# Hybrid decoder block: LRU, q, k and gate projections first, as 2x2 block products with seven multiplications

## The chip, the cores and the metric

The kernel runs on one core of a Trainium2 chip. The metric is the device time of one execution in microseconds (us); before the change it is 2504.58 us, the median of three runs. The engines are named as in the profile: PE (TensorE matmul), PEld (its weight load), DVE (VectorE), ACT (ScalarE), POOL (GpSimd) and SP (SyncE, whose queue starts nearly all DMAs here).

## The reference, cut to what matters

```python
D_MODEL = 1024; SEQ = 2048; N_HEADS = 8; HEAD_DIM = 64; V_DIM = 128
SPLIT_SIZES = (D_RNN, D_RNN, D_QK, D_QK, D_ATTN, D_ATTN, 2 * D_MODEL)   # 8192 columns
u = rmsnorm(h, pre_g[l])
z = jnp.einsum('bsd,df->bsf', u, w_in[l])
xr, zr, q, k, v, za, gm = jnp.split(z, split_points, axis=-1)
xc = causal_depthwise_conv(xr, conv_w[l], conv_b[l])
y_r = rg_lru(xc, ...) * jax.nn.silu(zr)            # recurrence over the 2048 positions
o = diff_attention(qh, kh, vh, lam)                # per head: softmax(q0 k0) - lam * softmax(q1 k1), causal, times v
o = rmsnorm(o, subln_g[l]) * (1.0 - lam_init)
y_a = o.reshape(B, S, D_ATTN) * jax.nn.silu(za)
g_r, g_a = jnp.split(jax.nn.sigmoid(gm), 2, axis=-1)
m = (g_r * jnp.einsum('bse,ed->bsd', y_r, w_br_rnn[l])
     + g_a * jnp.einsum('bse,ed->bsd', y_a, w_br_attn[l]))
h = h + rmsnorm(jnp.einsum('bsd,de->bse', m, w_out[l]), post_g[l])
```

## The kernel before, in words

Every product with weights is made in fp16 with two halves: a float32 value is scaled by a power of two and split into a high part and the rest, and high x high, high x rest and rest x high are summed in PSUM. So a projection of 128 output channels over 512 positions is 8 blocks of the inner dimension x 3 = 24 matmuls of 128x512 (`mm3`, L187 to L194). The normalised input lies in SBUF, transposed and split, as `uT` [128, 2, 8, 2048]; its 16 tiles of 128 positions are turned by two DMA transposes each (`x_fin`, L276), all issued from SP's queue.

The program has three stages.

1. The LRU stage. For 8 blocks of 128 channels `xr_half` and `zr_half` project half a row (1024 positions) of x_r and z_r, and convolution, gates (float32r matmuls L351 to L353), scan and gating run on DVE, ACT and POOL. The first three blocks are made in pieces of 128 positions (L302 to L304), so that the PE can start on each tile of the input as it comes.
2. The attention stage. An attention unit is one head and 128 queries (t = 0 to 15; unit t has t + 1 key blocks). `a_scores` makes the scores of the two softmaxes (ci = 0, 1) in pieces of up to 1024 keys (L814), and DVE copies each piece out of PSUM with its maximum (L826, with the mask L830). `a_exp` takes bias `nb` (L845) and the exponentials on ACT (L851). `a_comb` of the unit before joins the two softmaxes on DVE (L874), makes the high part on ACT (L876) and the rest on POOL (L877), and two DMA transposes per piece give `pt` (L880). `a_pv` multiplies `pt` with v two units later (L897, `LAG`), and after four units `a_norm` normalises. Between these parts the loop puts projection groups out of the list `fills`: k and q of 512 positions (`g_k`, `g_q`: 24 matmuls, a split on ACT and DVE (L667, L668), then DMAs that move the parts into `K` and `Q`), v and z_a of 256 positions (`g_va`: 48 matmuls of 128x256, L711) and the merge gates (`g_gm`: 24 matmuls and a tanh, stored to DRAM `gm_d`). A running count `acc` says how many groups are due in a unit, and `need` what a unit can't do without. Eight of the gate groups are kept for the end (`GM_T`).
3. The last stage, for two halves of the positions: the branch projections with the merge (`branch`, L1094) and the output projection with norm and residual (`final`, L1125).

Tile pools set which tile may be written when; a scheduler orders each engine's instructions when the program is built, so the order on an engine is not that of the source text. It is fixed at build time, and every engine runs its list in order.

Of the kernel before, what the change touches and what calls it, by code (L numbers as in the profile page):

```python
# [23 lines left out]
NH = 8  # L24
# [7 lines left out]
PD = 5     # x tiles loaded ahead  # L32
# [3 lines left out]
SEG_A = 2  # where a head's gate projections stand between its chunks  # L36
SEG_B = 5
# [11 lines left out]
def kernel(  # L49
# [35 lines left out]
    gm_d = drp.tile([2 * KD, 128, S], F32, name="gm_d")  # L85

# [3 lines left out]
    w16_p = ctx.enter_context(tc.tile_pool(name="w16", bufs=1))  # L90
# [3 lines left out]
    with ExitStack():  # L94
# [38 lines left out]
        def w16_at(i):  # L133
            """one of the four places for a block of weights"""
            return lambda w: w16_p.tile([128, 2, KD, 128], F16, tag=f"w{i % 4}", name="w16")

        def wkey_col(key):
            nm, h = key
            return {"k": C_K, "q": C_Q, "v": C_V, "za": C_ZA, "gm": C_GM}[nm] + h * 128
# [20 lines left out]
        def w_scale(w, ps, fac, keep=None):  # L160
            """power of two that brings the block's norm close to 2^13 (a rough sum is enough for it)"""
# [6 lines left out]
            if keep is None:  # L168
                w.cz = wn_p.tile([128, 1], F32, tag=f"w_cz_{w.tag}", name="w_cz",
                                 bufs={"wg": 4, "agm": 3}.get(w.tag, 2))  # L170
                nc.vector.scalar_tensor_tensor(out=w.cz, in0=w.iv, scalar=fac, in1=cu, op0=ALU.mult, op1=ALU.mult)

        def w_fin(w, ps, fac, dst, keep=None):
            if w.sg is None:
                w_scale(w, ps, fac, keep)
            w.t = dst(w)
            nc.scalar.activation(w.t[:, 0], w.st, AF.Identity, scale=w.sg)  # L177
            nc.vector.scalar_tensor_tensor(out=w.t[:, 1], in0=w.st, scalar=w.sg, in1=w.t[:, 0],  # L178
                                           op0=ALU.mult, op1=ALU.subtract)
            w.st = None  # L180

# [1 line left out]
        utx = ExitStack()  # L183
        utp = utx.enter_context(tc.tile_pool(name="utp", bufs=1))
        uT = utp.tile([128, 2, KD, S], F16, name="uT")

        def mm3(ps, w, c0, n):  # L187
            """ps[f128, n] += w^T u over all of d, s in [c0, c0 + n)"""
            i = 0
            for k in range(KD):  # L190
                for a, b in ((0, 0), (0, 1), (1, 0)):
                    nc.tensor.matmul(ps, w.t[:, a, k, :], uT[:, b, k, c0:c0 + n],  # L192
                                     start=(i == 0), stop=(i == 3 * KD - 1))
                    i += 1  # L194

        # ================= RG-LRU branch =================
        with ExitStack() as lx:
            le = lx.enter_context(tc.tile_pool(name="le", bufs=2))
            lp = lx.enter_context(tc.tile_pool(name="lp", bufs=2))
            ly = lx.enter_context(tc.tile_pool(name="ly", bufs=2))  # L200
            lc = lx.enter_context(tc.tile_pool(name="lc", bufs=1))
            tny[0] = lx.enter_context(tc.tile_pool(name="tnl", bufs=5))
            lps = lx.enter_context(tc.tile_pool(name="lps", bufs=3, space=PSUM))
            lpt = lx.enter_context(tc.tile_pool(name="lpt", bufs=2, space=PSUM))
# [7 lines left out]
            def load_g():  # L212
                gr = le.tile([KD, 128], F32, tag="rows", bufs=1, name="gr")
                nc.scalar.dma_start(out=gr, in_=pre_g[0].rearrange("(k p) -> k p", p=128))
                gb = lp.tile([128, D], F32, tag="a", name="gb")
                nc.sync.dma_start(out=gb, in_=pre_g[0:1, :].to_broadcast([128, D]))
                return gb, gr

            def prep_g(gr):
                """power of two that keeps the scaled, normalised input in fp16's range"""  # L220
                ss, tot = tl(1, "g_ss"), tl(1, "w_tot")
                jk = le.tile([KD, 128], F32, tag="idt", bufs=1, name="jg")
                nc.scalar.activation(jk, gr, AF.Square, accum_out=ss[0:KD])
                ps = lpt.tile([128, 1], F32, tag="tot", name="tot")
                nc.tensor.matmul(ps[:, 0:1], ones[0:KD, :], ss[0:KD], start=True, stop=True)
                nc.vector.tensor_scalar(out=tot, in0=ps[:, 0:1], scalar1=1e-30, scalar2=None, op0=ALU.max)
                pow2_bits(gi, tot, 10)
                pow2_inv(cu, gi)

            xts = {}  # L230
# [3 lines left out]
            def load_x(i):  # L234
                if i >= S // 128:
                    return
# [972 lines left out]
```

## Time and profile before

| | |
|---|---|
| time, three runs | 2504.58 us median (2501.92 to 2505.71) |
| profiled execution | span 2506.1 us from its first to its last instruction; no other time is recorded for it |
| PE busy | 2353.1 us (94% of the span) |
| DVE busy | 1548.4 us (62%) |
| ACT busy | 1224.6 us (49%) |
| POOL busy | 679.7 us (27%) |
| first matmul of a projection | 17.95 us |
| first attention score | 488.4 us |
| last product with v starts | 1956.9 us |
| first matmul of the branch projections | 1996.1 us |

A group of instructions in the profile reads: line, engine, operation, tile written <- tiles read, shape, count | busy time in us, mean ns of one | idle time of the engine just before them and what ended it. The mean of a matmul is its length from start to end, and matmuls overlap, so what one costs is the busy time over the count. A row of windows gives for a stretch of time the busy time of each engine with its number of instructions, the clock granted to TensorE (1.00 is full), the share of the DMA engines and GB/s.

### The profile page before, as it was taken

Reading aid. Unit: us, or ns where it says so; the run is one execution under the profiler, and the core shown is the slowest. Engines: PE = TensorE matmul, PEld = TensorE weight load, DVE = VectorE, ACT = ScalarE, POOL = GpSimd, SP = SyncE. Lnnn points to the kernel's source line nnn. Section 1 sums busy time; section 2 is a strip of 40 time slices with the busy share of each in tenths; the row PEclk is TensorE's granted clock in tenths of the full one; section 3 lists DMA queues with packets and bytes.
Section 4 is the critical chain, followed back from the end, with each engine's and each line's share of the span. In section 5 each row is a group of like instructions: output and inputs, shape, how many; then the busy total and the mean of one; then the engine's idle time right before and its main releaser. Section 6 shows DMA issues by size and latency. Waiting matters only on the chain. (4 is left out here: it accounts for less than half of the span.)

```text
span 2506.1 us, 41430 instructions
## 1 busy us (share of the span) xinstructions
PE 2353.1 (94%) x15240; PEld 1355.3 (54%) x15240; DVE 1548.4 (62%) x4316; ACT 1224.6 (49%) x2156; POOL 679.7 (27%) x415
## 2 busy tenths in 40 slices
PE   6789999999998999998998999999999899999998
PEld 5344444465665665665665655655655444444443
DVE  8877667668658566667567478468467244633323
ACT  5555545456547546556456457356456244312211
POOL 3443334212222212222222222223123133322211
PEclk9899999999999999999999999999999999999999
DMA  9511111235444534635535445445445854743202
GB/s 244 104 43 48 46 42 34 76 81 119 108 96 111 113 84 108 127 82 113 115 84 114 103 96 118 95 90 124 95 90 115 251 177 135 239 148 118 84 17 101
DMA packets 541323, 268.73 MB, mean 107 GB/s; under 512 B 370504, under 2 KB 518016, under 8 KB 541120
## 3 DMA queue, kind: packets, MB, share of 16 engines
q1 hardware_dynamic: 538144, 256.74, 42.6%
q0 software_dynamic: 2816, 9.08, 1.2%
q8 instruction: 119, 1.95, 0.3%
q14 instruction: 84, 0.69, 0.1%
q10 hardware_dynamic: 160, 0.27, 0.0%
HBM read 110.79 MB, written 41.94 MB: 61 GB/s over the span
## 5 line engine op out<-in xcount | busy, mean ns | idle before, releaser
L192 PEld LDWEIGHTS <-w 128*128 128x128 f16 x5040 | 475.9, 100 | 576.5 <-issue 89.2
L192 PE MATMUL mm<-uT,w 128*128 128x512 f16 x3072 | 705.1, 383 | 12.9 <-ACT gm L728 8.9
L877 POOL TENSOR_TENSOR e<-e,e 128x1024 f16<-128x1024 f32 (+2 forms) x192 | 317.0, 1666 | 970.6 <-ACT e L876 487.0
L851 ACT ACTIVATE e<-e,nb,sc_h 128x1024 f32<-128x1024 f32 (+7 forms) x384 | 376.1, 980 | 160.8 <-DVE nb L845 125.6
L826 DVE TENSOR_SCALAR_CACHE_REDUCE e<-sc 128x1024 f32<-128x1024 f32 (+7 forms) x352 | 305.2, 880 | 134.9 <-PE sc L814 122.3
L192 PE MATMUL ps<-uT,w 128*128 128x512 f16 (+1 forms) x1968 | 354.4, 345 | 26.1 <-ACT xr L318 17.7
L711 PE MATMUL mm<-wva,uT 128*128 128x256 f16 x3072 | 352.7, 275 | 3.3 <-DVE st L668 2.6
L1094 PE MATMUL psb<-yt,w 128*128 128x512 f16 x1536 | 332.9, 379 | 2.0 <-ACT w L177 1.5
L711 PEld LDWEIGHTS <-uT 128*128 128x128 f16 x3072 | 301.5, 99 | 48.8 <-issue 2.9
L814 PE MATMUL sc<-K,Q 128*128 128x512 f16 (+3 forms) x1280 | 287.2, 351 | 19.9 <-DVE e L826 13.8
L897 PE MATMUL o<-V,pt 128*128 128x128 f16 x3264 | 224.5, 222 | 38.4 <-DMA pt<-e 38.1
L1094 PEld LDWEIGHTS <-w 128*128 128x128 f16 x1536 | 149.1, 98 | 184.9 <-issue 3.9
L897 PEld LDWEIGHTS <-pt 128*128 128x128 f16 x3264 | 200.0, 99 | 72.8 <-DMA pt<-e 46.5
L876 ACT ACTIVATE e<-e 128x1024 f16<-128x1024 f32 (+2 forms) x192 | 150.1, 802 | 143.1 <-DVE e L874 118.5
L814 PEld LDWEIGHTS <-Q 128*128 128x128 f16 x1280 | 119.6, 99 | 133.2 <-issue 20.2
L874 DVE SCALAR_TENSOR_TENSOR e<-e,rs,e 128x1024 f32<-128x1024 f32 (+2 forms) x192 | 190.0, 1017 | 2.2
L1125 PE MATMUL psf<-wo,m 128*128 128x512 f16 x720 | 155.7, 379 | 0.0
L156 ACT ACTIVATE jk<-wst 128x1024 bf16<-128x1024 f32 x80 | 84.2, 1052 | 138.7 <-DMA wst<-in_w_in_dram 102.6
L1125 PEld LDWEIGHTS <-m 128*128 128x128 f16 x768 | 75.1, 98 | 90.6
L1098 DVE SCALAR_TENSOR_TENSOR t<-gt,psb 128x512 f32<-128x512 f32 x64 | 43.8, 686 | 120.2 <-PE psb L1094 100.1
L1148 ACT ACTIVATE jk<-psf 128x1024 bf16<-128x1024 f32 x15 | 15.4, 1024 | 134.0 <-PE psf L1125 69.4
L717 DVE SCALAR_TENSOR_TENSOR V<-mm,V 128x256 f16<-128x256 f32 x64 | 26.9, 421 | 85.7 <-ACT V L716 85.6
(247 smaller groups left out, 2417.3 us busy)
## 6 DMA issues: line engine op xcount, KB each, us to landing
wst<-in_w_in_dram SPq DMA_DIRECT2D x64, 512.0 KB, 4.5
xt<-in_x_dram SPq DMA_DIRECT2D x32, 512.0 KB, 4.5
gm_d<-gm SPq DMA_DIRECT2D x64, 256.0 KB, 2.7
gt<-gm_d SPq DMA_DIRECT2D x32, 512.0 KB, 3.8
K<-st SPq DMA_DIRECT2D x128, 64.0 KB, 2.0
Q<-st SPq DMA_DIRECT2D x64, 128.0 KB, 2.4
Q<-st SPq DMA_DIRECT2D x128, 64.0 KB, 2.1
ya_d<-yT SPq DMA_DIRECT2D x64, 128.0 KB, 2.0
```

Of the source, the lines that this page charges most:

```text
L156: nc.scalar.activation(jk, w.st, AF.Square, accum_out=ss)
L192: nc.tensor.matmul(ps, w.t[:, a, k, :], uT[:, b, k, c0:c0 + n], start=(i == 0), stop=(i == 3 * KD - 1))
L711: nc.tensor.matmul(ps[:, j, :], uT[:, a, k, s0:s0 + 128], wt[:, b, k].rearrange("p t f -> p (t f)"), start=(i == 0), stop=(i == 3 * KD - 1))
L814: nc.tensor.matmul(ps[:, x * 128:x * 128 + m], Qt[h, t // 4][:, v, ci, q0:q0 + 128], K[:, ci, 0:m], start=(v == 0), stop=(v == 1))
L826: nc.vector.tensor_scalar(out=ev[:, 0:m], in0=ps[:, 0:m], scalar1=1.0, scalar2=None, op0=ALU.mult, op1=ALU.max, accum_out=u.mx[:, ci, col: ...
L851: nc.scalar.activation(ev[:, 0:nb * 128], ev[:, 0:nb * 128], AF.Exp, bias=nb_[:, ci:ci + 1], scale=sc_h[h], accum_out=u.sm[:, pi, ci:ci + 1])
L874: nc.vector.scalar_tensor_tensor(out=e0[:, 0:m], in0=e1v[:, 0:m], scalar=rs, in1=e0[:, 0:m], op0=ALU.mult, op1=ALU.add)
L876: nc.scalar.activation(e1[:, 0, 0:m], e0[:, 0:m], AF.Copy)
L877: nc.gpsimd.tensor_tensor(out=e1[:, 1, 0:m], in0=e0[:, 0:m], in1=e1[:, 0, 0:m], op=ALU.subtract)
L897: nc.tensor.matmul(o, pt[:, a, kb % 8, :], V[:, kb % 4, b, :], start=(kb == 0 and i == 0), stop=(kb == n - 1 and i == 2))
L1094: nc.tensor.matmul(ps, w.t[:, p, k, :], y_t[b][:, q, k, sl], start=(i == 0), stop=(i == 3 * KD - 1))
L1125: nc.tensor.matmul(pn[n], m16[:, a, j, ms], wo[:, b, j, ns], start=(j == 0 and a == 0 and b == 0), stop=(j == KD - 1 and a == 1))
```

## The change

The projections of x_r, z_r, q, k and of all merge gates are made ahead of the attention, and v and z_a alone are left to the attention stage as groups between the units.

Two blocks of 128 output channels, two halves of the inner dimension (512 each) and two runs of 512 positions form a 2x2 block product. It is made with seven block products in place of eight, on sums and differences: of the weights (A11, A12, A22, S1 to S4) and of the input (B11, B21, B22 and T1 to T4). One block product is 4 x 3 = 12 matmuls of 128x512 (`prod`), so one group has 84. There are 24 pairs of channel blocks (8 for the LRU, 8 for k and q, 8 for the gates) and two halves of the positions (p = 0, 1), 48 groups. In a group, PSUM tile Y takes four products one upon the other and ACT copies it out three times on the way (`ev`); Z takes two, X one, and DVE adds the copies to X and Z (`add_to`).

The input is kept as `uK[p]` (B11, B21, B22) and `uM[p]` (T1 to T4) for each half. For two tiles of positions that belong together (`u_pair`), four split tiles are made and turned by eight DMA transposes, two of them half as wide as the others; the block B12, which only v and z_a need, goes to DRAM (`b12_d`) and is turned and read back (`ub12`) when the first stage is over. k and q are stored to DRAM (`kq_d`), and the heads load `K` and `Q` from there (`load_kq`), four units ahead. The high parts of k, q and v are scaled by 2^-12 (`SH`), not 2^-14. The weights lie in tiles of half a block (`wq`, ten buffers), also in the last stage.

```diff
-GM_T = 8
 LAG = 2
-ACC0 = 8.0
+ACC0 = 4.0
...
+        uK = [utp.tile([128, 2, 12, CH], F16, name=f"uK{p}") for p in range(2)]
...
+            uM = [um.tile([128, 2, 16, CH], F16, name=f"uM{p}") for p in range(2)]
...
+            def u_pair(p, i):
...
+                ua = u_split(a, nc.gpsimd)
+                for l in range(2):
+                    nc.sync.dma_start_transpose(out=uK[p][:, l, 0:8, sl], in_=ua[:, l])
+                ub = u_split(b, nc.vector)
+                for l in range(2):
+                    nc.sync.dma_start_transpose(out=uK[p][:, l, 8:12, sl], in_=ub[:, l, CH:D])
+                    nc.sync.dma_start(out=b12_d[l, p * CH + i * 128:p * CH + (i + 1) * 128, :], in_=ub[:, l, 0:CH])
...
+                ua = u_split(a, nc.vector)
+                for l in range(2):
+                    nc.sync.dma_start_transpose(out=uM[p][:, l, 0:8, sl], in_=ua[:, l])
+                ub = u_split(b, nc.gpsimd)
+                for l in range(2):
+                    nc.sync.dma_start_transpose(out=uM[p][:, l, 8:16, sl], in_=ub[:, l])
...
+            pairs = [pair_of("G", 0), pair_of("K", 0), pair_of("L", 0)]
+            for i in range(1, KD):
+                pairs += [pair_of("L", 1)] if i == 1 else []
+                pairs += [pair_of("G", i), pair_of("K", i)]
+                if i + 1 < KD:
+                    pairs += [pair_of("L", i + 1)]
...
+            def prod(ps, r, p, a, b, start, stop):
+                t, k0 = ublk(p, b)
+                q = r.q[a]
+                i = 0
+                for k in range(4):
+                    for x_, y_ in ((0, 0), (0, 1), (1, 0)):
+                        nc.tensor.matmul(ps, q[:, x_, k, :], t[:, y_, k0 + k, :], start=start and i == 0,
+                                         stop=stop and i == 11, skip_group_check=True)
+                        i += 1
...
+            def g_P1(g):
+                g.Y = pY.tile([128, CH], F32, tag="Y", name="psY")
+                prod(g.Y, g.r, g.p, "A11", "B11", True, True)
+                g.y1 = ev(g.Y)
+            def g_P56(g):
+                g.Z = pZ.tile([128, CH], F32, tag="Z", name="psZ")
+                prod(g.Z, g.r, g.p, "S1", "T1", True, True)
+                prod(g.Y, g.r, g.p, "S2", "T2", False, True)
+                g.u2 = ev(g.Y)
+            def g_P27(g):
+                X = pX.tile([128, CH], F32, tag="X", name="psX")
+                prod(X, g.r, g.p, "A12", "B21", True, True)
+                add_to(g, 0, X, g.y1)
+                prod(g.Y, g.r, g.p, "S3", "T3", False, True)
+                u3 = ev(g.Y)
+                add_to(g, 3, g.Z, u3)
+            def g_P43(g):
+                prod(g.Y, g.r, g.p, "A22", "T4", False, True)
+                c_use(g, 2, g.Y)
+                prod(g.Z, g.r, g.p, "S4", "B22", False, True)
+                add_to(g, 1, g.Z, g.u2)
...
-            def g_k(h, c):
-            def g_q(h, c):
-            def g_gm(f, c):
+            def load_kq(h, c):
+                s0 = c * CH
+                t = kp.tile([128, 2, CH], F16, tag="K", name="K")
+                for l in range(2):
+                    nc.sync.dma_start(out=t[64 * l:64 * l + 64], in_=kq_d[0, h, l, :, s0:s0 + CH].rearrange(
+                        "(i p) s -> p i s", i=2))
...
             def chunk_groups(h, c):
-                return [("k", h, c), ("q", h, c), ("va", h, c, 0), ("va", h, c, 1)]
+                return [("va", h, c, 0), ("va", h, c, 1)]
...
+            fills = W_(0) + chunk_groups(0, 0) + chunk_groups(0, 1)
             for h in range(NH):
+                fills += chunk_groups(h, 2) + chunk_groups(h, 3) + W_(h + 1)
                 if h + 1 < NH:
+                    fills += chunk_groups(h + 1, 0) + chunk_groups(h + 1, 1)
...
-            per = (len(fills) - ntail - 8) / float(NH)
+            per = (len(fills) - 4) / float(NH)
+            load_kq(0, 0)
             fill_to(need[0, 0])
             for i, u in enumerate(units):
                 fill_to(need[u.h, u.t // 4])
+                if u.t % 4 == 0 and i + 4 < len(units):
+                    load_kq(units[i + 4].h, units[i + 4].t // 4)
```

Two places of the build order show how the change moves instructions. The first is SP's queue while the input is made ready. `uT`, `uK0`, `uM0` are written by DMA transposes out of split tiles `u16`, `xt` are tiles of the input, `b12_d` is the block in DRAM. Before:

```order
L240 DMA xt_215<-in_x_dram 128x1024
L276 DMA_TRANSPOSE uT_82<-u16_212 128x8x128
L276 DMA_TRANSPOSE uT_82<-u16_260 128x8x128
L276 DMA_TRANSPOSE uT_82<-u16_268 128x8x128
L240 DMA xt_263<-in_x_dram 128x1024
```

and with the change, for one pair of tiles:

```order
L235 DMA xt_359<-in_x_dram 128x1024
L235 DMA xt_361<-in_x_dram 128x1024
L262 DMA_TRANSPOSE uK0_84<-u16_404 128x8x128
L265 DMA_TRANSPOSE uK0_84<-u16_409 128x4x128
L262 DMA_TRANSPOSE uK0_84<-u16_404 128x8x128
L266 DMA b12_d_61<-u16_409 128x512
L265 DMA_TRANSPOSE uK0_84<-u16_409 128x4x128
L266 DMA b12_d_61<-u16_409 128x512
L277 DMA_TRANSPOSE uM0_91<-u16_425 128x8x128
L262 DMA_TRANSPOSE uK1_85<-u16_549 128x8x128
L274 DMA_TRANSPOSE uM0_91<-u16_420 128x8x128 x2
L277 DMA_TRANSPOSE uM0_91<-u16_425 128x8x128
```

Where two transposes stood for a tile, eight stand for a pair of tiles, and two stores beside them.

The second place is the PE's list in a late unit of a head (t = 14). `sc` are scores, `mm` are projections (L192 before), `o` is the product with v. Before, with weight loads left out:

```order
L814 MATMUL sc_10513<-K_9718,Q_9824 128x384
...
L192 MATMUL mm_10619<-uT_82,w16_10030 128x512
...
L897 MATMUL o_10563<-V_8417,pt_10348 128x128
...
L192 MATMUL mm_10619<-uT_82,w16_10030 128x512
...
L814 MATMUL sc_10539<-K_8147,Q_9824 128x512
...
L814 MATMUL sc_10546<-K_9718,Q_9824 128x384
```

and with the change, from the second softmax of t = 13 to that of t = 14:

```order
L862 MATMUL sc_20762<-K_18823,Q_20160 128x512
...
L945 MATMUL o_20401<-V_20042,pt_20667 128x128
...
L862 MATMUL sc_20769<-K_20157,Q_20160 128x256
...
L862 MATMUL sc_20861<-K_18823,Q_20160 128x512
...
L862 MATMUL sc_20868<-K_20157,Q_20160 128x384
...
L945 MATMUL o_20918<-V_19216,pt_20753 128x128
...
L862 MATMUL sc_20894<-K_18823,Q_20160 128x512
```

The 20 projection matmuls between the scores of the first and of the second softmax are gone, and no group of v and z_a stands in the units t = 11 to 14 of this head: its eight groups stand in t = 2 to 10.

More of the change, by code (lines that the diff above doesn't have):

```diff
@@ L210 @@
             gi = cst.tile([128, 1], F32, name="gi")
[L212 to L228, printed above, removed]
@@ L243 @@
[L243 to L254 removed]
+            gr = evp.tile([KD, 128], F32, tag="Y", name="gr")
+            nc.scalar.dma_start(out=gr, in_=pre_g[0].rearrange("(k p) -> k p", p=128))
@@ L280 @@
-            order = [(C_XR if i % 2 == 0 else C_ZR) + (i // 2) * 128 for i in range(2 * KD)]
-            ahead = [("k", 0), ("q", 0), ("v", 0), ("za", 0)]
-            order += [wkey_col(k) for k in ahead]
-            ws = {}
-            def wld(i):
-                ws[i] = w_load(win, order[i], tag="wg" if i < 2 * KD else "a" + ahead[i - 2 * KD][0])
-            def wstat(i):
-                w_stat(ws[i])
-            def wfin(i):
-                w_fin(ws[i], lpt.tile([128, 1], F32, tag="tot", name="tot"), 0.5 if i % 2 and i < 2 * KD else 1.0,
-                      w16_at(i))
@@ L311 @@
[L311 to L325 removed]
+                a, b = xts.pop(n), xts.pop(n + 1)
@@ new lines, in g_P43, with after, tick @@
+            def g_P43(g):
[3 more added lines that the diff above has]
+                add_to(g, 1, g.Z, g.u2)
+            later = []
+            clock = [0]
+            def after(n, f):
+                later.append((clock[0] + n, f))
+            def tick():
+                clock[0] += 1
+                for e in [e for e in later if e[0] <= clock[0]]:
+                    later.remove(e)
+                    e[1]()
@@ L454 @@
-            x_stat(6, 2)
-            x_fin(6, 2, gb)
-            wld(3)
-            x_stat(8, 2)
-            x_fin(8, 2, gb)
-            wstat(3)
-            wfin(3)
-            prm_ps = lpt.tile([128, 65], F32, tag="tot", name="prm_ps")
+            gb = lp.tile([128, D], F32, tag="y", name="gb")
+            nc.sync.dma_start(out=gb, in_=pre_g[0:1, :].to_broadcast([128, D]))
+            for n in range(2, 4):
+                load_x(n)
+            p_load(pairs[0])
+            load_x(4)
@@ new lines @@
+            g_ss, g_tot = tl(1, "g_ss"), tl(1, "w_tot")
+            g_jk = evp.tile([KD, 128], F32, tag="Y", name="g_jk")
+            nc.scalar.activation(g_jk, gr, AF.Square, accum_out=g_ss[0:KD])
+            g_ps = gps(1)
+            nc.tensor.matmul(g_ps, ones[0:KD, :], g_ss[0:KD], start=True, stop=True)
+            nc.vector.tensor_scalar(out=g_tot, in0=g_ps, scalar1=1e-30, scalar2=None, op0=ALU.max)
+            pow2_bits(gi, g_tot, 8)
+            pow2_inv(cu, gi)
+            u_pair(0, 0)
@@ new lines, with u_blk @@
+            while later:
+                tick()
+        ubp = utx.enter_context(tc.tile_pool(name="ubp", bufs=1))
+        ub12 = [ubp.tile([128, 2, 4, CH], F16, name=f"ub12{p}") for p in range(2)]
+        for p in range(2):
+            for l in range(2):
+                for i in range(4):
+                    nc.sync.dma_start_transpose(out=ub12[p][:, l, :, i * 128:(i + 1) * 128],
+                                                in_=b12_d[l, p * CH + i * 128:p * CH + (i + 1) * 128, :])
+        def u_blk(l, k, s0):
+            p, c, o = s0 // HALF, (s0 // CH) % 2, s0 % CH
+            if c == 0:
+                return uK[p][:, l, k, o:o + 128]
+            return uK[p][:, l, 4 + k, o:o + 128] if k >= 4 else ub12[p][:, l, k, o:o + 128]
@@ L594 @@
             ps_m = ax.enter_context(tc.tile_pool(name="ps_m", bufs=2, space=PSUM))
-            wl = {k: ws[2 * KD + i] for i, k in enumerate(ahead)}
+            wl = {}
             wva_t = {}
```

671 lines of the change are left out of this document (324 added, 347 removed).

## The prediction

> **What bounds the kernel now.** I read the page, then windows by stage, then groups and waits inside the attention, then the timeline at the joints.
>
> ```profile
> span 2506.1 us, 41430 instructions
> PE 2353.1 (94%) x15240; PEld 1355.3 (54%) x15240; DVE 1548.4 (62%) x4316; ACT 1224.6 (49%) x2156; POOL 679.7 (27%) x415
> 0.00:120.00 120.00, 76.78 (x726) 56.75 (x727) 100.14 (x253) 61.95 (x86) 42.94 (x38) 0.90 0.82 180
> 120.00:488.00 368.00, 347.49 (x1556) 168.30 (x1554) 264.19 (x307) 197.69 (x186) 137.09 (x72) 0.97 0.13 41
> 488.00:1975.00 1487.00, 1415.31 (x10577) 897.91 (x10578) 974.61 (x3230) 834.30 (x1700) 364.43 (x228) 0.98 0.49 107
> 1975.00:2506.00 531.00, 513.56 (x2384) 232.32 (x2382) 209.48 (x528) 130.63 (x185) 135.26 (x77) 0.99 0.43 138
> ```
>
> The windows are start, the rest of the LRU stage, attention, last stage; the columns PE, PEld, DVE, ACT, POOL, clock, DMA share, GB/s. The PE is 94% to 97% busy in every stage but the start. In the attention DVE works 975 of 1487 us, and that is hidden because the PE has projections to do meanwhile:
>
> ```profile
> L192 PE MATMUL mm<-uT,w 128*128 128x512 f16 x3072 | 705.1, 383 | 12.9 <-ACT gm L728 8.9
> L192 PE MATMUL ps<-uT,w 128*128 128x512 f16 (+1 forms) x1968 | 354.4, 345 | 26.1 <-ACT xr L318 17.7
> L711 PE MATMUL mm<-wva,uT 128*128 128x256 f16 x3072 | 352.7, 275 | 3.3 <-DVE st L668 2.6
> L1094 PE MATMUL psb<-yt,w 128*128 128x512 f16 x1536 | 332.9, 379 | 2.0 <-ACT w L177 1.5
> L814 PE MATMUL sc<-K,Q 128*128 128x512 f16 (+3 forms) x1280 | 287.2, 351 | 19.9 <-DVE e L826 13.8
> L897 PE MATMUL o<-V,pt 128*128 128x128 f16 x3264 | 224.5, 222 | 38.4 <-DMA pt<-e 38.1
> DVE e L826 <- PE sc L814: 122.3, 79, 4.8
> DVE s L862 <- ACT e L851: 83.0, 39, 5.1
> ```
>
> The 3072 matmuls `mm` (k, q, gates), 705 us, lie between the attention's own work. The last two rows (who waited for whom in the attention: total, times, longest) say that DVE waits for scores and exponentials and the PE hardly for DVE.
>
> **The change part by part.**
>
> *Fewer products.* 4608 matmuls of 512 columns (3072, and 1536 for x_r and z_r) become 48 x 84 = 4032. The 576 saved cost between 0.217 us (L1094: 332.9 / 1536) and 0.2365 us (LRU stage: 368 / 1556, all waits in it): 125 to 136 us off the PE. That is the whole gain; what follows is what stands against it.
>
> *The first stage.* It has 4032 + 192 gate matmuls. I take 0.2365 us each, since the LRU work that set that rate runs here too: 999 us; at 0.217 it would be 917. Not all can run from the start: the order has group 1 (p = 0), 12 matmuls of the next pair, and then products on `uK1`, `uM1`, which exist when the last of 16 input tiles is turned. Before, the PE started on the first tile:
>
> ```profile
> 17.95 0.26 PE L192 MATMUL ps<-uT,w 128*128 128x128 f16 x1 [2.90 <-DMA uT<-u]
> 13.40 1.35 SPq L276 DMA_TRANSPOSE uT<-u  x1
> 71.88 25.88 SPq L276 DMA_TRANSPOSE uT<-u  x10
> uT<-u SPq DMA_TRANSPOSE x32, 4.9
> ```
>
> 32 transposes took SP from 13.4 to 97.8 us, 2.64 us each with the input loads between them, and the last landed 4.9 us later. With the change there are 48 whole and 16 half ones, 56 wholes: 13.4 + 56 x 2.64 + 4.9 = 166 us. If SP's 1.35 us for one is the price, 64 of them end at 105 us: the lower bound. I take 166: the ten of the second row stand with almost nothing between them and still took 2.6 us.
>
> The Trainium skill, DMA: Bandwidth & Descriptors, section Latency and other measured facts, gives 261 GB/s for a DMA transpose; by that one of these (256 KB) would take an estimated 1.0 us, 56 of them 56 us, and the stage and the sum would be 92 us shorter. The rows above stand against it.
>
> Until 166 us the PE can do some 120 matmuls (28 us). The stage then ends at 166 + 999 - 28 = 1137 us; 1137 against 488 before. The conversions (`ev`, `add_to`) go beside the PE: one group has six of them at about 0.7 us in 19.9 us. What is late if that cover is gone is a rival below.
>
> *The joint.* The 16 half transposes of B12 wait for the end of the stage, and the loads of K and Q stand behind them on SP; weights of v and z_a have to be split. At 1.35 us the 16 take 22 us, and two groups of v on the first chunk (2 x 48 x 0.115 = 11 us) go meanwhile. No row shows it; ends 0 and 30 us, I take 12.
>
> *The attention.* Taken out: 1536 matmuls of k and q, most of the gates' 1536, and on DVE
>
> ```profile
> L668 DVE SCALAR_TENSOR_TENSOR st<-mm,st 128x512 f16<-128x512 f32 x61 | 41.7, 685 | 54.5 <-ACT st L667 54.5
> L178 DVE SCALAR_TENSOR_TENSOR w<-wst,w_sg_agm,w 128x1024 f16<-128x1024 f32 x16 | 23.8, 1487 | 0.8 <-ACT w L177 0.7
> L178 DVE SCALAR_TENSOR_TENSOR w<-wst,w_sg_ak,w 128x1024 f16<-128x1024 f32 x7 | 9.5, 1355 | 0.2 <-ACT w L177 0.2
> L178 DVE SCALAR_TENSOR_TENSOR w<-wst,w_sg_aq,w 128x1024 f16<-128x1024 f32 x7 | 8.9, 1278 | 0.1
> L164 DVE TENSOR_SCALAR w_tot<-tot 128x1 f32<-128x1 f32 x44 | 6.7, 153 | 3.0 <-PE tot L162 3.0
> ```
>
> that is 42 + 24 + 18 us, and some 30 us of small steps (30 blocks x 7 x 0.15). DVE keeps 975 - 114 = 861 us. The PE keeps 353 + 287 + 225 = 864 us. And one unit waits for the one before: bias, exponentials, join, maxima of the second softmax, next bias. Where little is projected, the spacing of the biases shows that loop:
>
> ```profile
> 1397.41 0.28 DVE L845 TENSOR_SCALAR nb<-mx,nsc_h,lsp 128x2 f32<-128x2 f32 x1
> 1400.86 0.29 DVE L845 TENSOR_SCALAR nb<-rm,nsc_h,lsp 128x2 f32<-128x2 f32 x1
> 1548.31 0.28 DVE L845 TENSOR_SCALAR nb<-rm,nsc_h,lsp 128x2 f32<-128x2 f32 x1
> 1558.68 0.29 DVE L845 TENSOR_SCALAR nb<-rm,nsc_h,lsp 128x2 f32<-128x2 f32 x1
> 1530.00:1560.00 30.00, 25.45 (x186) 14.64 (x185) 25.66 (x81) 20.12 (x38) 8.45 (x5) 0.94 0.60 122
> ```
>
> 3.45 us from t = 0 to 1, 10.4 us from t = 14 to 15; the mean, 6.9 us, over 128 units is 886 us. So the stage has three floors of nearly one height, 861, 864 and 886 us, and no spare work to lay over the gaps of each: in t = 11 to 14 no v or z_a is left, and the PE has there some 0.44 us per key block (287 + 225 us over 8 x 136), 5 to 7 us a unit, against 9 to 10.4 us of the loop. The window above, t = 13 to 15 of one head, is the stretch of before nearest to this: DVE was busy 25.66 of 30 us, 86%. I take that share for the stage: 861 / 0.86 = 1001 us, against 1487 before. Ends: 886 (the loop alone) and 1148 (DVE busy 75%).
>
> *The last stage.* Before, eight gate groups filled the time in which the last unit is normalised, stored and read back:
>
> ```profile
> 1954.38 2.74 PE L897 MATMUL o<-V,pt 128*128 128x128 f16 x46
> 1962.82 2.50 SPq L929 DMA_TRANSPOSE yT<-y  x2
> 1970.42 5.45 SPq L1025 DMA_DIRECT2D yt<-yr_d  x4
> 1996.08 12.00 PE L1094 MATMUL psb<-yt,w 128*128 128x512 f16 x54 [1.50 <-ACT w L177]
> yt<-yr_d SPq DMA_DIRECT2D x8, 1024.0 KB, 10.1
> ```
>
> That cover is gone. From the end of the last product (1957.1) to the issue of `yt` are 13.3 us and 10.1 more to its landing: 23 us of idle PE. From 1996.1 the stage runs 510 us as before. 533 us; ends 520 and 545.
>
> *Sum:* 1137 + 12 + 1001 + 533 = 2683 us of span. The span of the profiled execution, 2506.1 us, is 1.5 us over the median of the three runs (2504.58), so the time is about 2682 us, 177 us slower.
>
> **The rivals.**
>
> *The PE stays the bound (faster).* The first stage at 0.217 us: 166 + 917 - 26 = 1057; the attention at the loop's floor, 886; a joint hidden; 525 for the rest: 2468 us. For it speaks that the PE was never short of work before; against it that DVE reached 86% in a stretch where the PE still had projections. It decides where first score and attention together take less than 1967 us (2500 - 533). Chance 0.07.
>
> *Both stages better than I take, yet slower.* Ramp at 130 us and attention at 920 us (DVE 94%): 2566 us. Chance 0.17. With it the gain just fails to pay for ramp and idle gaps.
>
> *DVE holds up the first stage.* In the LRU stage DVE worked 264 of 368 us, for about 13 of 16 half rows some 20 us each; a group with 84 matmuls has 19.9 us of PE. In the 16 LRU groups DVE also has `add_to` (3 x 0.7) and weights to split, and the PE waits for X and Z behind convolution and scan. 5 us in each of 16 groups: 80 us, 2762 us. Against it: the 32 other groups leave DVE two thirds idle, and work is put off over later groups. Chance 0.13.
>
> *The clock falls.* With gaps on the PE the granted clock drops:
>
> ```profile
> 71.00:98.00 27.00, 18.30 (x72) 0.00 (x0) 0.82 0.67 127
> ```
>
> 0.82 while the PE waited for transposes. If it fell to 0.82 in t = 0 to 10, where the PE has about 61 us a head (29 us of its own, 32 us of v and z_a), that would be 13 us a head, 104 us: 2786 us. Against it: 0.94 in the window of t = 13 to 15. Chance 0.06.
> By the Trainium skill, TensorE: Matmul & The Clock Gate, section What's actually happening, the array runs at half clock after an idle window of about 3.4 us and at full clock after as long a busy one; the gaps of 4 us per late unit are at that limit, which is why this rival has a chance.
>
> **How the numbers follow.** The forecast of 2682 us has 0.57. Its own range is 2600 to 2770 (ramp -60, attention -80 to +70, the rest 20). To hold eight in ten I reach down to 2550, past the better case (2566), and up to 2830, past both slower rivals; out are the faster rival and the tail in which both slower ones meet (2866). 0.2% is about what a measurement of this kernel can tell from no change. Faster 0.07, same 0.02 (a point between the faster rival and the better case), slower 0.91.
>
> **What would show it.** In the profile of the changed kernel: about 4032 matmuls on a line of their own at 0.22 to 0.24 us each; PE nearly idle between 100 and 165 us, released by DMA into `uK1` and `uM1`; the first score near 1150 us; the attention about 1000 us long with PE near 85% and DVE 86% busy; in t = 11 to 14 PE waiting for DVE or `pt`; 20 us without PE work ahead of the branch projections. I am wrong if the first score comes before 1060 us, or if the attention takes less than 900 us or the PE is busy there for over 95%.

## The result and the profile after

The changed kernel takes 2839.81 us (median of 4 runs, 2839.17 to 2842.4), the kernel before 2504.38 us (4 runs) on the same chip: ratio 1.1348, 95% interval 1.1332 to 1.1364. It is slower by 335 us, where 177 were forecast, and just outside the range that ended at 2830.

The head of the page, and the windows by stage (columns as before: PE, PEld, DVE, ACT, POOL busy, clock, DMA share, GB/s). The cuts are at the start of free running in the first stage, its last product, the first score, the last product with v, and the first branch projection:

```profile
span 2837.6 us, 40496 instructions
PE 2322.2 (82%) x14232; PEld 1303.8 (46%) x14232; DVE 1828.7 (64%) x4715; ACT 1383.1 (49%) x2524; POOL 912.4 (32%) x563
```
```profile
0.00:154.00 154.00, 36.79 (x124) 14.46 (x125) 113.27 (x253) 71.35 (x101) 72.41 (x54) 0.88 0.77 185
154.00:1139.00 985.00, 920.85 (x4155) 423.02 (x4154) 576.21 (x954) 481.07 (x720) 345.79 (x206) 0.97 0.21 67
1139.00:1165.00 26.00, 19.46 (x150) 15.90 (x150) 7.15 (x23) 5.12 (x10) 0.00 (x0) 0.87 0.55 128
1165.00:2304.00 1139.00, 842.88 (x7483) 623.02 (x7482) 907.48 (x2906) 683.50 (x1466) 358.80 (x225) 0.88 0.54 109
2304.00:2326.00 22.00, 1.11 (x9) 0.69 (x5) 8.33 (x43) 9.75 (x23) 3.05 (x2) 0.57 0.81 258
2326.00:2838.00 512.00, 501.12 (x2320) 226.74 (x2320) 216.25 (x536) 132.26 (x206) 132.34 (x76) 0.99 0.41 133
```

The first stage ends at 1139 us (forecast 1137), the joint is 26 us (12), the last stage 22 + 512 (533 in all). The attention is 1139 us where 1001 were forecast: 138 of the 155 us by which the span exceeds the forecast's 2683. The PE's busy time went down by only 31 us over the whole program (2353.1 before), its share from 94% to 82%: in the attention it was busy 95% of the stage before, and is 74% now, at a granted clock of 0.88 instead of 0.98.

Two views of the attention stage say who works and who waits. First groups (busy, mean ns, idle time before them and what ended it), then waits (total, times, longest):

```profile
L945 PE MATMUL o<-V,pt 128*128 128x128 f16 x3264 | 258.4, 236 | 187.9 <-DMA pt<-e 183.8
L874 DVE TENSOR_SCALAR_CACHE_REDUCE e<-sc 128x1024 f32<-128x1024 f32 (+7 forms) x352 | 306.2, 880 | 86.5 <-PE sc L862 55.8 <-POOL e L925 18.1 <-DMA pt<-e 8.8
L922 DVE SCALAR_TENSOR_TENSOR e<-e,rs,e 128x1024 f32<-128x1024 f32 (+2 forms) x192 | 209.5, 1119 | 1.2
L893 DVE TENSOR_SCALAR nb<-rm,nsc_t,lsp 128x2 f32<-128x2 f32 x120 | 67.4, 561 | 1.8
```
```profile
PEld L945 <- DMA pt<-e: 230.0, 113, 11.7
PE o L945 <- DMA pt<-e: 183.8, 85, 9.3
ACT e L899 <- DVE nb L893: 144.1, 60, 9.6
ACT e L924 <- DVE e L922: 137.0, 84, 4.7
DVE s L910 <- ACT e L899: 58.5, 35, 5.1
```

The largest wait of the PE is new: the product with v (L945) waits 184 us for the transposed weights `pt`, against 38 us before. ACT waits 144 us for `nb` and 137 us for the join L922; DVE waits for ACT's exponentials. No engine is near full. The timeline of one late stretch shows how a single step spreads:

```profile
1984.46 2.35 DVE L922 SCALAR_TENSOR_TENSOR e<-e,rs,e 128x1024 f32<-128x1024 f32 x2
...
1988.87 5.26 DVE L922 SCALAR_TENSOR_TENSOR e<-e,rs,e 128x1024 f32<-128x1024 f32 x2
...
1990.38 9.65 POOL L925 TENSOR_TENSOR e<-e,e 128x1024 f16<-128x1024 f32 x4 [0.41 <-ACT e L924]
...
1994.05 1.83 DVE L960 TENSOR_TENSOR v<-v 128x4 f32<-128x4 f32 x1
...
1996.00 0.16 PE L161 MATMUL tot<-w_s,ones 128*128 128x1 bf16 x1 [13.13 <-DVE w_s L157]
```

Two joins take 2.35 us with POOL idle and 5.26 us while POOL works; a step on 128x4 elements takes 1.83 us beside it; the PE, next in whose queue stands the norm of a weight block, is idle for 13.13 us.

### The profile page after: what moved, and what is told of

Read it like the earlier page. It is cut to its first block, busy times and chain, and to the rows that moved or that the text cites. A ratio compares the mean times of both kernels' runs of the same rounds, so it can differ in the third digit from the quotient of the medians.

```text
span 2837.6 us, 40496 instructions
## 1 busy us (share of the span) xinstructions
PE 2322.2 (82%) x14232; PEld 1303.8 (46%) x14232; DVE 1828.7 (64%) x4715; ACT 1383.1 (49%) x2524; POOL 912.4 (32%) x563
## 5 line engine op out<-in xcount | busy, mean ns | idle before, releaser
L356 PEld LDWEIGHTS <-wq 128*128 128x128 f16 x4032 | 396.7, 100 | 601.2 <-issue 144.3
L899 ACT ACTIVATE e<-e,nb,sc_t 128x1024 f32<-128x1024 f32 (+7 forms) x384 | 376.1, 980 | 191.2 <-DVE nb L893 144.1
L356 PE MATMUL psY<-uM,wq 128*128 128x512 f16 x1728 | 416.6, 393 | 32.7 <-ACT Y L362 30.2
L945 PE MATMUL o<-V,pt 128*128 128x128 f16 x3264 | 258.4, 236 | 187.9 <-DMA pt<-e 183.8
L874 DVE TENSOR_SCALAR_CACHE_REDUCE e<-sc 128x1024 f32<-128x1024 f32 (+7 forms) x352 | 306.2, 880 | 86.5 <-PE sc L862 55.8
L1144 PE MATMUL psb<-yt,wq 128*128 128x512 f16 x1536 | 335.5, 381 | 14.8 <-DMA yt<-yr_d 14.8
L945 PEld LDWEIGHTS <-pt 128*128 128x128 f16 x3264 | 223.1, 106 | 251.6 <-DMA pt<-e 230.0
L788 PE MATMUL mm<-wva,uK 128*128 128x256 f16 x2304 | 294.7, 277 | 13.0 <-ACT wva L173 8.3
L788 PEld LDWEIGHTS <-uK 128*128 128x128 f16 x2304 | 226.7, 100 | 55.2 <-issue 17.4
L1144 PEld LDWEIGHTS <-wq 128*128 128x128 f16 x1536 | 150.1, 98 | 197.6 <-issue 20.1
L922 DVE SCALAR_TENSOR_TENSOR e<-e,rs,e 128x1024 f32<-128x1024 f32 (+2 forms) x192 | 209.5, 1119 | 1.2
L174 DVE SCALAR_TENSOR_TENSOR wq<-wst,w_sg_p,wq 128x512 f16<-128x512 f32 x168 | 144.0, 889 | 101.3 <-ACT wq L173 100.9
L356 PE MATMUL psY<-uK,wq 128*128 128x512 f16 x576 | 138.1, 388 | 35.6 <-DMA uK<-u 34.2
L356 PE MATMUL psZ<-uM,wq 128*128 128x512 f16 x576 | 140.7, 388 | 4.8 <-DMA uM<-u 2.5
L356 PE MATMUL psX<-uK,wq 128*128 128x512 f16 x576 | 140.7, 385 | 4.3 <-DVE xr L367 4.3
```

What stands on the lines that cost most here:

```text
L174: nc.vector.scalar_tensor_tensor(out=q[:, 1], in0=src, scalar=sg, in1=q[:, 0], op0=ALU.mult, op1=ALU.subtract)
L356: nc.tensor.matmul(ps, q[:, x_, k, :], t[:, y_, k0 + k, :], start=start and i == 0, stop=stop and i == 11, skip_group_check=True)
L788: nc.tensor.matmul(ps[:, j, :], u_blk(a, k, s0), wt[:, b, k].rearrange("p t f -> p (t f)"), start=(i == 0), stop=(i == 3 * KD - 1))
L874: nc.vector.tensor_scalar(out=ev[:, 0:m], in0=ps[:, 0:m], scalar1=1.0, scalar2=None, op0=ALU.mult, op1=ALU.max, accum_out=u.mx[:, ci, col: ...
L899: nc.scalar.activation(ev[:, 0:nb * 128], ev[:, 0:nb * 128], AF.Exp, bias=nb_[:, ci:ci + 1], scale=sc_t[:, h:h + 1], accum_out=u.sm[:, pi, ...
L922: nc.vector.scalar_tensor_tensor(out=e0[:, 0:m], in0=e1v[:, 0:m], scalar=rs, in1=e0[:, 0:m], op0=ALU.mult, op1=ALU.add)
```

## The experiments

All are changes of the changed kernel. "Stage" is the attention from the first score to the end of the last product with v: 1139 us there, at 2839.8 us in all. Runs without a named interval are single runs; four runs of the changed kernel lie within 3 us. The edits of e3 to e6, e8, e11 and e13 to e15 leave out work or data that the block needs, and e12 makes one product twice: they price a part and are no versions to use.

**Does the PE's order bind? e1, e2.** The wait for `pt` suggested theory A: in the build order, the product with v of unit i stands ahead of the second-softmax scores of unit i+2, so a late transpose holds up those scores, hence maxima, bias, exponentials and the next joins. e1 has the edit below; e2 has it with `LAG = 3`, so that the product follows the scores of the unit three later, and with the tile counts that its expectation names.

```
-                        a_pv(units[i - LAG])
+                        with tc.issue_after(u.mm.ins):     # u.mm: last score matmul of unit i
+                            a_pv(units[i - LAG])
```


> Only the order on PE is changed: a unit's product with v is queued behind all score products of the unit two later, where the changed kernel has it behind those of the first softmax alone. Theory A (a loop over two units: join, copy, rest, transposes, product with v, the second scores of the unit two later, maxima, exponentials, join): that loop now spans three units, the waits of L945 on pt fall to a third or less, the stage from 1165 to 2307 shrinks by 80 to 120 us, the time is 2720 to 2760. Theory B (DVE, stretched beside POOL, is what binds): the stage stays within 20 us, the time is 2820 to 2860.

> As the run before, with the product queued behind all scores of the unit three later, six pt tiles in place of four, and five K, nine wq, five t4 and three tna tiles in place of six, ten, six and four for their room. Theory A: the loop spans four units and another one binds; 0 to 40 us less than the run before, 2690 to 2750. Theory B: unchanged, 2820 to 2860.

e1 took 2857.45 us (stage 1159), e2 2824.45 us (stage 1136; of its 15 us less, 3 are the stage's, the first stage ends 21 us earlier, the step into the last one is 3 shorter and the last takes 12 longer). The wait for `pt` falls from 184 us to 49 in e1 and 23 in e2, and another one stands there instead (rows of e2):

```profile
1144.00:2281.00 1137.00, 827.65 (x7475) 624.26 (x7475) 901.95 (x2905) 680.72 (x1468) 363.25 (x225) 0.87 0.53 109
```
```profile
PE sc L862 <- DVE e L874: 215.5, 60, 13.1
PE o L945 <- DMA pt<-e: 22.7, 18, 7.1
```

The same idle time has moved to another releaser (in the changed kernel `sc` waits 47 us for L874). As the cause, theory A fell: the largest wait on the page was not what set the pace. Why e1's stage is 20 us longer is open.

**What is POOL's subtraction worth? e3, e4.**

```
                     for hl_ in range(2):
-                        nc.sync.dma_start_transpose(out=pt[:, hl_, 0:nb, :], in_=e1[:, hl_, 0:m])
+                        nc.sync.dma_start_transpose(out=pt[:, hl_, 0:nb, :], in_=e1[:, 0, 0:m])
-                    nc.gpsimd.tensor_tensor(out=e1[:, 1, 0:m], ..., op=ALU.subtract)      # e4 only
```


> POOL computes the low half of the softmax weights as before (L925), but the second transpose takes the high half again, so the product with v no longer waits for POOL (the output lacks the low half). Theory A: 2.3 to 4.6 us go out of the two-unit loop, 1.2 to 2.3 us per unit in 40 to 64 units: 48 to 147 us less, 2690 to 2790. Theory B: POOL and DVE work beside each other as before, 2820 to 2860.

> As the run before, and L925 is left out altogether, so POOL is nearly idle in the attention stage. Theory A: within 25 us of the run before, 2665 to 2790. Theory B: the run before is unchanged and this one is not: DVE's 908 us busy fall to the 861 forecast, and the stage to 861/0.8 = 1076 us, 66 less: about 2775, with the whole gain against the run before in this step.

e3: 2814.04 us, stage 1113 (26 less). e4: 2768.42 us, stage 1064 (75 less). So a third of it is the wait for POOL, and two thirds go only when POOL does not work at all. For e3 theory A had too much (48 to 147) and theory B nothing; e4 is near theory B's figure, 2775 and a stage of 1076; whether theory B's reason holds is the question of e17 below. Window and DVE groups of e4:

```profile
1170.00:2234.00 1064.00, 833.58 (x7482) 615.62 (x7483) 784.46 (x2906) 680.60 (x1466) 41.71 (x33) 0.90 0.57 116
```
```profile
L874 DVE TENSOR_SCALAR_CACHE_REDUCE e<-sc 128x1024 f32<-128x1024 f32 (+7 forms) x352 | 306.9, 880 | 141.9 <-PE sc L862 83.1 <-DMA pt<-e 51.8 <-ACT e L924 2.2
L922 DVE SCALAR_TENSOR_TENSOR e<-e,rs,e 128x1024 f32<-128x1024 f32 (+2 forms) x192 | 183.6, 983 | 0.9
L893 DVE TENSOR_SCALAR nb<-rm,nsc_t,lsp 128x2 f32<-128x2 f32 x120 | 34.2, 285 | 1.7
```

With POOL's subtraction in place, `nb` takes 561 ns on average instead of 285, the join 1119 instead of 983; the maxima L874, which read PSUM, 880 in both. DVE's busy time falls by 123 us, the stage by 75. The Trainium skill, SBUF — State Buffer, section Who interferes with whom, has a rule that fits which steps stretch: a VectorE step with two SBUF inputs, or in a two-port mode, shares its interface with GpSimd, and one with at most one SBUF input and no such mode does not. The three rows agree (the page puts `tensor_scalar`, the form of `nb`, among the two-port candidates).

**Is it the loop through `nb`? e5, e6, and is there PE slack? e8.**

```
-    AF.Exp, bias=nb_[:, ci:ci + 1],                                   # e5; e6: with e4's edit
+    AF.Exp, bias=lsp,
-    for i, (a, b) in enumerate(((0, 0), (0, 1), (1, 0))):             # e8, the product with v
+    for i, (a, b) in enumerate(((0, 0),)):
```


> The exponentials take a constant as their bias instead of nb, so they follow the first maxima pass over their own scores and no longer wait for the last maxima and nb (the maxima and nb are still computed; the weights are not shifted by their maximum). Theory L (the loop nb, exponentials, join, maxima, nb sets the pace of the attention stage): its longest step is out, the stage of 1139 us falls to DVE's own 908 us busy over 0.95, about 960 to 1010, the time to 2660 to 2710. Theory P (DVE's own work, stretched beside POOL, sets it): at most 40 us less, 2800 to 2840. Theory E (PE at its lower clock, with the waits for pt, sets it): within 20 us, 2820 to 2860.

> The run before and L925 left out together (the second transpose takes the high half again). Leaving out L925 alone took the stage from 1139 to 1064 us. Theory L: both gains add, DVE's 786 us busy or PE's 843 sets the stage, about 890 to 940, the time 2590 to 2650. Theory P: close to the run without L925 alone, 2740 to 2770. Theory E: likewise 2740 to 2770.

> The product with v is computed with one of its three matmuls, high half by high half (the output lacks the cross terms): 2176 matmuls less, two thirds of L945's 258 us, 172 us of PE's 843 in the attention stage. Theory L and theory P: PE has slack, at most 40 us less, 2800 to 2840. Theory E: 100 to 200 us less, 2640 to 2740.

e5: 2752.36 us, e6: 2710.42, e8: 2792.89. Their windows, one each:

```profile
1163.00:2217.00 1054.00, 821.37 (x7481) 617.37 (x7481) 884.26 (x2906) 695.58 (x1466) 347.00 (x225) 0.91 0.58 117
```
```profile
1168.00:2176.00 1008.00, 821.58 (x7480) 606.64 (x7481) 777.60 (x2906) 689.86 (x1466) 41.06 (x33) 0.93 0.61 123
```
```profile
1170.00:2259.00 1089.00, 745.00 (x5308) 500.67 (x5308) 890.08 (x2906) 681.59 (x1466) 364.42 (x225) 0.83 0.55 113
```

Freeing the exponentials from `nb` brings 85 us, with POOL's part 131. Both are more than theories P or E allow and less than theory L hoped for (960 to 1010, 890 to 940). In e8 2176 matmuls fewer bring 50 us, between theories L and P (at most 40) and theory E (100 to 200). The PE's busy time falls by 98 and not by 172: at a clock of 0.83 the scores, the same 1280 matmuls, are busy for 348 us instead of 320, and the product with v keeps 111 us of its 258 where a third would be 86. So each of three engines' parts is a piece of the chain, and none is the chain.

**Does it matter where the V/z_a groups stand? e9, e10.** The edit is `ACC0 = 4.0` to 6.0 and to 8.0.

> ACC0, the lead of the V/za groups over the units, goes from 4 to 6. In the changed kernel the order on PE has no V/za matmul beside the units t = 11 to 15 of the later heads, and one lump of 94 behind the next head's first scores; with 6 they stand in small pieces beside t = 12 to 15 in all heads but head 6. Theory F (where these matmuls stand decides: beside long units they fill PE's waits, in the lump they hold up DVE and ACT): every head but head 6 takes about what the changed kernel's first two take, 132 to 135 us, the stage of 1139 us falls to 1060 to 1100, the time to 2760 to 2800. Theories L and P (loop, DVE beside POOL): within 20 us, 2820 to 2860.

> ACC0 8, as the kernel before had it: the pieces stand from t = 10 on, in all heads. Theory F: as the run before or a little less, 2740 to 2800. Theories L and P: 2820 to 2860.

2812.37 us (stage 1117) and 2819.02 us (stage 1122). A better spread brings 22 and 18 us of the stage, about half of the least that theory F gave (1139 - 1100 = 39); both times lie a little under the 2820 to 2860 of theories L and P.

**Was the order a second, hidden bound? e13, e14, e15.** e2's order with e4's, e5's, and both edits.

> The product queued behind the scores of the unit three later (with its tiles as in that run), and L925 left out. Alone they took the attention stage from 1139 us to 1136 and 1064. Theory A with L (two loops of nearly the same pace, one around nb, one around the transposes and PE's order: each hides what the other's removal brings): 990 to 1035. If PE's wait for the transposes holds nothing up in any combination: within 20 us of 1064.

> The product queued behind the scores of the unit three later, and the constant bias. Alone: 1136 and 1054 us. Theory A with L: both loops are open, DVE's 884 us busy beside POOL sets the stage, 930 to 1000. If PE's wait for the transposes holds nothing up: within 20 us of 1054.

> All three: the product three units later, the constant bias, no L925. Without the first: 1008 us. Theory A with L: nothing is left but the engines' own work, PE's 820 us or DVE's 780 over 0.95, 850 to 920. If PE's wait for the transposes holds nothing up: within 20 us of 1008.

```profile
1150.00:2214.00 1064.00, 818.29 (x7474) 616.44 (x7472) 785.78 (x2905) 678.30 (x1465) 40.98 (x33) 0.89 0.59 116
```
```profile
1147.00:2198.00 1051.00, 815.63 (x7475) 616.32 (x7475) 898.08 (x2905) 694.40 (x1465) 349.77 (x225) 0.90 0.60 118
```
```profile
1146.00:2129.00 983.00, 815.47 (x7474) 617.03 (x7471) 780.58 (x2905) 689.05 (x1467) 43.51 (x33) 0.92 0.64 126
```

2753.24, 2738.45 and 2669.61 us. With either of the other causes in place the order is worth nothing (1064 and 1064, 1051 and 1054); with both away it is worth 25 us (983 against 1008). In e13 and e14 that is the case in which the PE's wait for the transposes holds nothing up; e15's 983 fits neither of its two cases (850 to 920, or within 20 us of 1008).

**Is a stretched `nb` the path? e17, e18.** Nothing is left out here. e18 adds the edit to e16, which is below.

```
-    nc.vector.tensor_scalar(out=nb_, in0=rm, scalar1=nsc_t[:, h:h + 1], scalar2=lsp, op0=ALU.mult, op1=ALU.add)
+    nc.scalar.activation(nb_, rm, AF.Identity, scale=nsc_t[:, h:h + 1], bias=lsp)
```


> Only nb moves: 128 steps of 128x2 elements go from DVE to ACT (an Identity with the same scale and bias). Nothing is left out. On DVE nb took 0.285 us with POOL idle and 1.11 us on average beside POOL (45 of 128), 67 us in all; the maxima that feed it come from an operation that was not stretched (rm: 153 ns with L925, 152 without). If POOL's hold on DVE lies on the path from the maxima to the exponentials: 30 to 80 us off the stage of 1139, the time 2760 to 2810. If nb's stretch costs nothing on the path, or ACT's queue gives it back (ACT is 60% busy, and nb then stands behind copies and squares): within 20 us of 2840.

```profile
1164.00:2302.00 1138.00, 842.48 (x7484) 625.52 (x7484) 847.14 (x2778) 727.07 (x1595) 365.16 (x225) 0.87 0.53 109
```
```profile
L893 ACT ACTIVATE nb<-rm,lsp,nsc_t 128x2 f32<-128x2 f32 x120 | 45.9, 383 | 148.1 <-DVE rm L890 148.0
```

2837.52 us (4 runs; ratio to the kernel before 1.1326, interval 1.1302 to 1.135). DVE, the busiest engine, lost 60 us of work, and the stage stayed: ACT now waits 148 us for `rm` where it waited 144 us for `nb`. So what ACT waits for is mostly DVE's work ahead of the bias (maxima, joins), not the bias step itself. The run isn't a clean test of DVE's time, though: ACT, in the same chain, got 44 us more work (684 to 727 us), and the second case of the expectation allows for that. Which of POOL's effects made the 49 us between e3 and e4 is left open. Of the 123 us by which DVE's busy time fell in e4, `nb` has 33, the joins have 26 (209.5 - 183.6) and other small steps the remaining 64; DVE's waits for tiles that POOL still reads (18.1 us, row L874) are a further candidate.

**The gate projections back between the units: e7, e16, e18.** Pairs G go out of the first stage, and each head gets plain groups of 24 matmuls, the last eight behind the last unit:

```
-            pairs = [pair_of("G", 0), pair_of("K", 0), pair_of("L", 0)]
+            pairs = [pair_of("K", 0), pair_of("L", 0)]
...
+            def g_gm(f, c):      # 24 matmuls of 512 columns, tanh, store to gm_d
```


> The gate projections go back into the attention stage as plain groups of 24 matmuls between its units, with the last eight behind the last unit; LRU, q and k stay in seven products. Out of the first stage: 16 groups x 84 x 0.2365 us = 318 us; into the attention: 64 x 24 x 0.2365 = 363 us. If the idle PE time there (1142 - 843 = 299 us) takes them, PE (843 + 363 = 1206 us) sets the stage at 1220 to 1290, the 19 us at its end are covered, the granted clock there is above 0.95, and the time is 2580 to 2670. If the waits stay beside them (the loop goes on setting the pace and the groups lengthen it), the stage is 1400 to 1500 and the time 2780 to 2880.

> The gate projections back in the attention stage as plain groups, and the product queued behind the scores of the unit three later; no work is left out. With the gates back alone the stage took 1218 us with PE 1106 busy, the time was 2705. If PE's waits for the transposes are a part of its 112 us idle: 1150 to 1190, time 2640 to 2680. If not: within 20 us of 1218, 2690 to 2725.

> nb on ACT together with the gate projections back in the attention and the product three units later; nothing is left out. Without nb on ACT: stage 1156 us with PE 1081 busy, time 2625. PE is at 94% there, so at most 30 us less whatever nb does: 2595 to 2635; more than 20 us less only if PE's idle 75 us are waits for nb.

e16 is e7 with e2's order and tiles, and e18 is e16 with `nb` on ACT. e7: 2705.43 us. e16: 2625.24 us. e18: 2603.72 us (4 runs; 1.0395 of the kernel before, interval 1.0368 to 1.0421), the fastest version found and still slower than the kernel before. Windows of the stage in e7, e16 and e18:

```profile
942.00:2160.00 1218.00, 1105.98 (x8962) 746.90 (x8961) 929.95 (x3036) 756.40 (x1589) 359.81 (x225) 0.96 0.52 121
```
```profile
916.00:2071.00 1155.00, 1080.79 (x8960) 742.25 (x8960) 928.81 (x3035) 755.49 (x1588) 353.40 (x225) 0.98 0.60 128
```
```profile
912.00:2048.00 1136.00, 1073.85 (x8966) 740.97 (x8967) 867.02 (x2907) 797.87 (x1716) 355.78 (x225) 0.99 0.61 130
```

This is the plainest answer to where the time went. e16 against e2 (same order, same tiles): 253 us more PE work in the stage, all gate groups but the last eight, cost 20 us there (1156 against 1136). Between the units the gate projections are nearly free; in the first stage they cost 232 us (its last product ends at 886 instead of 1118). The steps into the attention and out of it are longer, by 3 and 19 us, and the last stage is 9 us shorter: in all 199 us. k and q were not put back. In e18 the first score comes 424 us later than in the kernel before (912 against 488) and the stage is 333 us shorter (1136 against 1469); what of the 99 us that are left is theirs was not tried. Here, with the PE 94% busy, order does bind (63 us from e7 to e16) and `nb` on ACT too (20 us of stage; I had put e18 at 2595 to 2635).

Two expectations were missed: e7's time (2580 to 2670), for its first stage ended at 916, not at 821; and e16's time, 15 us under its 2640 to 2680, while its stage was within 1150 to 1190. In e7's first stage the PE waits for the LRU's steps; one row, its longest wait 13.3 us:

```profile
PE psZ L356 <- DVE C L367: 29.1, 6, 13.3
```

**The first stage: e11, e12.**

```
-                for l in range(2):                                     # e11, transposes into uM[p]
+                for l in range(2 if p == 0 else 0):
-                prod(X, g.r, g.p, "A12", "B21", True, True)            # e12
+                prod(X, g.r, g.p, "A12", "B21", True, False)
+                prod(X, g.r, g.p, "A12", "B21", False, True)
```


> The 16 transposes into uM of the second half of the tokens are left out, and the products of that half read the first half's uM (the output is not the reference's). If the ramp is set by its DMA transposes, as the prediction had it, 12 to 16 transposes at about 2.4 us go out of it: the first stage ends 25 to 40 us before 1139, the time is 2800 to 2815. If arithmetic on DVE, ACT and POOL sets the ramp: within 10 us of 2840.

> The product of A12 and B21 is computed twice into the same bank (an eighth product in each of 48 groups, 576 matmuls; the output is not the reference's). If PE sets the first stage, as the prediction had it, 576 x 0.2365 = 136 us more: its end at 1260 to 1280, the time 2960 to 2980. If the LRU's chain or DVE sets a part of it (with the gate projections taken out it ended at 916 where PE alone gives 821): 40 to 100 us more, 2880 to 2940.

e11: 2844.56 us; the last product ends at 1131.7 instead of 1139, 7 us earlier. Its window from 100 to 150 us, and that of the changed kernel:

```profile
100.00:150.00 50.00, 21.87 (x75) 8.40 (x74) 40.25 (x66) 21.27 (x28) 22.51 (x12) 0.67 0.57 148
```
```profile
100.00:150.00 50.00, 19.17 (x64) 7.32 (x63) 37.23 (x66) 21.45 (x28) 20.05 (x11) 0.67 0.82 198
```

The DMA share falls from 0.82 to 0.57 and the PE gets 11 matmuls more: these transposes were not the limit. DVE is the busiest engine in that window; that it is the limit was not tried.

e12: 2915.28 us; the last product ends at 1212.3, 73 us later for 576 more matmuls:

```profile
154.00:1212.00 1058.00, 1027.11 (x4727) 473.02 (x4726) 603.65 (x954) 481.70 (x722) 358.22 (x207) 0.99 0.20 63
```

1058 / 4727 = 0.224 us each at 97% busy, against 985 / 4155 = 0.237 at 93%. The eighth product partly fills waits that the seven leave. Saving it is worth 73 us of time, not 125 to 136.

## Why the prediction was right and wrong

*First stage, 1137 us: right (1139), with one reason wrong.* The rate of 0.2365 us held (0.237). The ramp, 166 us by DMA transposes, was over at 154, when the last of them was issued, but e11 shows that the last 16 hold it up by only 7 us, where 2.64 us each would be 42: this term came near by luck. Its price was misread. The row of ten transposes in 25.88 us was taken to have almost nothing between them; the waits of SP's queue in the kernel before say that it stood still in there:

```profile
SPq L276 <- ACT u L269: 9.9, 1, 9.9
SPq L276 <- POOL mask L520: 2.3, 1, 2.3
```

So 12 of the 26 us went by in waiting, 9.9 of them for a split tile `u`. In the changed kernel, where tiles are ready, four transposes in a row are issued 1.3 us apart (from 121.57 to 125.61 us), the price that the prediction had set aside as its lower bound. The Trainium skill, DMA: Bandwidth & Descriptors, section Latency and other measured facts, gives 261 GB/s for a DMA transpose, by which one takes an estimated 1.0 us; the 1.3 us lie nearer to that than to 2.64. No run here times a transpose by itself.

*"125 to 136 us off the PE. That is the whole gain."* The matmuls are gone, but e12 prices them at 73 us, because the first stage has waits of its own (the PE is idle for 64 of the 985 us, in e12 for 31 of 1058).

*Rival "DVE holds up the first stage".* Small in the changed kernel: waits that end with a DVE step are 36 of the PE's 64 idle us. With the gate groups gone (e7) the stage ends 95 us behind the 821 worked out for the PE alone, 6 us for each of 16 LRU groups, near the 5 us priced. That the gate groups hid it is what the pair suggests; the waits were not tested one by one.

*Joint, 12 us: 26.* Inside its ends (0 to 30).

*Attention, 861 / 0.86 = 1001 us: this is the step that failed; it took 1139.* Two parts of it, and the method, were off. DVE's busy time was 907 us, not 861: the joins took 209.5 us where they had taken 190 before, `nb` 67 where it had taken 56, and e4 shows that such steps are longer with POOL's subtraction than without. At 86% that alone gives 907 / 0.86 = 1055. And the share was 80%: 1139. The share came from 30 us of one head in which the PE still had projections (51 of its 186 matmuls); it was carried to a stage from which those had been taken. The method was to divide the busiest engine's time by a share, and the share did not stay: it is 80% in the changed kernel, 74% in e4 (784 of 1064 us) and in e17 (847 of 1138). The pace is a chain over engines: bias, exponentials, join, maxima, bias on one side (85 us when cut, while DVE's busy time falls by only 23), POOL's subtraction on the other (75 us), 131 together, 156 with the PE's order as well; two thirds of the product with v are worth 50. With the first two away the stage takes 1008 us, about what was forecast for it with both in place. The floors (861, 864, 886) were counted as if each loop ran alone. What keeps e15 at 983 us, with PE 815 and DVE 781 busy, is not settled. One reading is off without effect: the PE's own work, 287 + 225 us over 8 x 136 key blocks, is 0.47 us per block, not 0.44.

*Last stage: right.* 22 us without PE work (23 forecast), 512 (510).

*Rival "the clock falls".* The clock fell to 0.88 over the stage, but in other units than the rival had it. In t = 0 to 10 it was 0.80 in the second head and 0.91 to 0.97 in the others; in t = 11 to 15, where few or no projections are left, it was 0.77 to 0.79 in the last five heads. The sixth head, cut at the bias of t = 11:

```profile
1854.60:1941.30 86.70, 72.62 (x672) 55.84 (x671) 72.47 (x257) 50.74 (x122) 23.76 (x18) 0.94 0.50 103
1941.30:1998.90 57.60, 27.63 (x221) 17.32 (x220) 46.48 (x123) 37.55 (x67) 24.26 (x13) 0.77 0.56 112
```

The PE's busy time, 843 us, stayed below the forecast's 864. Over the whole stage the clock goes with the PE's busy share: 0.83 in e8 (68%), 0.88 in the changed kernel (74%), 0.96 in e7 (91%), 0.98 in e16 (94%). What it costs by itself, and what of it is an effect of the waits, was not separated.

*The direction* was right for the stated reason: work that had been nearly free beside the attention's waits was given a stage of its own. For the gates e16 shows it (199 us); for k and q it is argued. "In t = 11 to 14 PE waiting for DVE or `pt`" and "20 us without PE work" are in the trace.

## What to carry to other kernels

Price work by what it costs at its place: 253 us of PE time between the attention units cost 20 us, and the gate projections in a PE-bound stage cost 232 us, though there they needed an eighth fewer multiplications. When cover is taken from a stage of short steps that wait for each other, don't divide the busiest engine's time by a share seen while the cover was there: follow one unit's chain across the engines, with the durations that its steps have beside each other. And a long wait on the page is not yet a cause: removing the PE's largest wait, or a stretched step, only renamed it as long as the other links of the chain stood.

## What was not expected of the hardware

A VectorE step on 128x2 elements, 0.285 us with POOL idle, took up to 2.09 us and 1.11 us on average in the 45 of 128 cases in which POOL was at work; a join of 128x1024 went from 1.28 to as much as 3.15 us. The maxima over PSUM did not stretch (880 ns in both).

Fewer matmuls do not shorten the PE's busy time in proportion: in e8 29% fewer (7483 to 5308) came with 12% less busy time (843 to 745 us) and a clock of 0.83 instead of 0.88.
